# Differential heads in a fixed order, with spread transposes and ScalarE's sums of squares, and x added to the projection's first half by transfers

## The chip, the cores and the metric

The kernel runs on one core of a Trainium2 chip. The metric is the time of one execution in device microseconds (us). The kernel before took 655.91 us, the median of three runs (654.86 to 656.41). A profile of one execution gives each engine's instructions. TensorE (PE) multiplies matrices and transposes; VectorE (DVE), ScalarE (ACT) and GpSimd (POOL) work on tiles; SyncE's queue (SP) starts transfers. Matmuls write PSUM, which is used here as eight banks of 128 x 512 floats.

## The reference

One residual block on x, 512 tokens of 1024 features, all in float32:

```python
h = rms_norm(x, attn_norm_g)
z = h @ w_in                       # latent q, kv, rope key | differential q, k, v
y_mla  = mla_group(...)            # 8 heads of 64
y_diff = diff_group(...)           # 4 heads of 128
x = x + concat([y_mla, y_diff]) @ w_out
x = x + conv_ffn(rms_norm(x, ffn_norm_g), ...)
x = x + sigmoid(rms_norm(x, ple_norm_g) @ w_ple_gate) * (p @ w_ple_proj)
```

A differential head has two maps of logits, m = 0 and 1, each from 64 features. Both get the same bias by distance and a mask by chunks of 64 tokens. The head's output is `(softmax(l0) - lam * softmax(l1)) @ v`, and each token's 128 outputs are then divided by their root mean square and scaled by a gain.

## The kernel before, in words

**Products in three parts.** TensorE multiplies in a reduced float32 (`F32R`). Each operand is split in a high half (a cast on ScalarE, `split` L183, L186; weights L148) and a low half (what the cast lost, on VectorE, L184, L187, L149). `mm3` (L152) adds three products: high by high, high by low, low by high. A weight comes through `load_w` (L143): a transfer of 512 KB into one of three `raw` tiles, a cast, a subtraction. There are five pairs of `hi` and `lo` tiles.

**Stages.** The projections of x come first, then the eight latent heads, then the four differential heads with most of the output projection, the rest of that projection, the feed-forward part and the gate. The change lies in the differential stage, from about 152 to 240 us of the span.

**The differential stage.** The loop at L767 goes over 16 places: head h of 4, query block t of 4. A place (h,t) has t + 1 key blocks, since later ones are masked. TensorE's order is the program's order:

- logits of the place two ahead, both maps (`diff_logits`, L662), each map in its own bank of tag `lg` (three banks);
- at t = 0, the transposes of the next head's keys (`diff_T(h + 1, 1)`, L654), and after the products of this place those of its queries (`diff_T(h + 1, 0)`);
- one or two filler units (`pump`, by the table `FILL_DIFF`);
- transposes of this place's probabilities (`probs_T`, L533) into a bank of tag `tp` (two banks, which all transposes of the stage share), copied to `pt` by ScalarE;
- products with the values of the place before (`diff_pv`, L685), into one bank `ob` for each head;
- at t = 2, the transposes of the head before's outputs, with their split (`y_split`, L613).

`diff_logits` also issues what follows from the logits. For each map VectorE adds the bias and takes the negated maximum (L675), and ScalarE the exponential with its sum (L676). VectorE then puts both maps together (reciprocal L680, factor L681, combination L682). The `pm` tiles that hold the maps are four.

At a head's end `diff_pv` squares its 512 columns on ScalarE (L696), copies them to `yd` (L697), sums the squares by token on VectorE (L699), takes a power on GpSimd (L704) and scales `yd` on VectorE (L706).

**The filler.** `wo_units` (L638) is the output projection as a generator. Its first half takes y blocks 0 to 3 (the latent heads): for eight blocks b of 128 output features, two units of two y blocks each; the finished block is added to x by VectorE (`add_x`, L631), which frees one of two `acc` banks. The second half takes y blocks 4 to 7: for b = 0 to 3 one unit with blocks 4 and 5 is in the filler. The rest comes after the loop in two rounds (L802 to L899). The first round takes blocks 4 to 6, beginning with block 6 for b = 0. The second adds block 7, which is the last head's. The tiles of x are loaded by SyncE's queue in the last latent head (`load_x`, L712).

**Order on the other engines.** PE is under `manual_schedule`: it runs in program order. For VectorE, ScalarE and GpSimd this holds only inside marked regions, and from L736 to L847 there is none: a planner orders their instructions by its own estimate of when each is ready. There a later weight's cast can run ahead of an earlier copy, and does. `issue_after` puts single instructions behind others by hand.

Of the kernel before, what the change touches and what calls it, by code (L numbers as in the profile page):

```python
# [62 lines left out]
FILL_DIFF = ((2, 1, 1, 1), (1, 1, 2, 1), (1, 2, 2, 1), (1, 1, 2, 2))  # L63
# [31 lines left out]
def hybrid_block(ctx: ExitStack, tc: tile.TileContext, a: dict, out: bass.AP):  # L95
# [537 lines left out]
    wo2 = {}  # L633

    def wo_w(kq, dq):
        return load_w(a["w_out"][kq, dq], 1024, f"o{kq}{dq}")

    def wo_units(kq, dqs, nk):  # L638

        for dq in dqs:  # L640
            w = wo_w(kq, dq)
            if kq:
                wo2[dq] = w
            for b in (2 * dq, 2 * dq + 1):
                ps = bank("acc", f"o{kq}{b}")
                for k in range(0, nk, 2):
                    mm3(ps, wo_blocks(4 * kq + k, 4 * kq + k + 2, b, w), k == 0, k == nk - 2)
                    if k == nk - 2:
                        add_x(b, ps)
                    yield  # L650
# [3 lines left out]
    def diff_T(h, c):  # L654
        ps = bank("tp" if h else "acc", f"d{c}T{h}")
        for t in range(NT):
            TE.transpose(ps[:, tsl[t]], zd[c][t][:, h * P:(h + 1) * P], ident)
        h_, l_ = st[4 * (h % 2) + 2 * c], st[4 * (h % 2) + 2 * c + 1]
        split(h_, l_, ps, dcol if c == 0 else None)
        df["qk", h, c] = (h_, l_)  # L660

    def diff_logits(h, t):  # L662
# [3 lines left out]
        s0 = df["s0", h][:, t:t + 1]  # L666
        (qh_, ql_), (kh_, kl_) = df["qk", h, 0], df["qk", h, 1]
        pms, s1 = [], sm.tile([P, 1], F32, tag="s1", bufs=4, name="s1")
        for m in range(2):
# [3 lines left out]
            pm = pm_tile("pmd")  # L673
            nm = sm.tile([P, 1], F32, tag="nm", bufs=4, name="nmd")
            V.tensor_tensor_reduce(out=pm[:, :n], in0=ps[:, :n], in1=strips[0][:, h, T - n:], scale=1.0, scalar=3e38, op0=ALU.add, op1=ALU.min, accum_out=nm)  # L675
            S.activation(pm[:, :n], pm[:, :n], AF.Exp, bias=nm, scale=-1.0, accum_out=s0 if m == 0 else s1)  # L676
            pms.append(pm)

        cf = sm.tile([P, 1], F32, tag="cf", bufs=4, name="cf")
        V.reciprocal(cf, s1)  # L680
        V.scalar_tensor_tensor(cf, cf, nlam, s0, op0=ALU.mult, op1=ALU.mult)  # L681
        V.scalar_tensor_tensor(pms[0][:, :n], pms[1][:, :n], cf, pms[0][:, :n], op0=ALU.mult, op1=ALU.add)  # L682
        df["pm", h, t] = pms[0]

    def diff_pv(h, t):  # L685
        if t == 0:
            df["po"] = bank("ob", f"do{h}")
        po, pt = df["po"], df.pop(("pt", h, t))
        for j in range(t + 1):
            TE.matmul(po[:, tsl[t]], pt[:, tsl[j]], zd[2][j][:, h * P:(h + 1) * P], start=j == 0, stop=j == t)  # L690
        if t < NT - 1:
            return
        s0 = df["s0", h]
        yn = tt(f"yd{h}")
        sq = sq_tile("sqo")[:, :T]
        S.activation(sq, po, AF.Square)  # L696
        df["copy"] = S.copy(yn, po)  # L697
# [7 lines left out]
        yv = yn.rearrange("p (t d) -> p t d", d=P)  # L705
        df["scale"] = V.tensor_tensor(yv, yv, ro.unsqueeze(2).broadcast_to([P, NT, P]), op=ALU.mult)  # L706
        df["y", h] = yn
# [4 lines left out]
    def load_x():  # L712
# [3 lines left out]

    last_mla = [
        lambda: diff_T(0, 0),
        lambda: diff_T(0, 1),
# [42 lines left out]
    diff_logits(0, 0)  # L762
    mla_pv(*slots[-1])
    diff_logits(0, 1)
    pump()
    y_split(3, ymn[3], None, "tp")
    for i, (h, t) in enumerate(dslots):  # L767
        if i + 2 < len(dslots):
            diff_logits(*dslots[i + 2])
        if h + 1 < DH and t == 0:  # L770
            diff_T(h + 1, 1)
# [4 lines left out]
        if h + 1 < DH and t == 0:  # L776
            diff_T(h + 1, 0)
        if h and t == 2:
            y_split(4 + h - 1, df["y", h - 1], ocol, "tp")
# [10 lines left out]
    for dq in (2, 3):  # L790
        wo2[dq] = wo_w(1, dq)

    pk = kvp.tile([P, 4, 1024], F32R, tag="kv", name="pk")
    for i, (src, name) in enumerate(((a["pT"], "pT"), (a["w_pp"][0], "pp0"))):
        raw = load_raw(src, 1024, name)
        S.copy(pk[:, 2 * i], raw)
        with tc.issue_after(df["scale"].ins):
            V.tensor_tensor(pk[:, 2 * i + 1], raw, _f32(pk[:, 2 * i]), op=ALU.subtract)
# [3 lines left out]
    for b in order[:6]:  # L802
        n = len(early)
        if n == 5:
            y_split(7, df["y", 3], ocol, "tp")
# [27 lines left out]
    def behind_head(src, tag, name, bufs=1):  # L833

        h_, l_ = (ffn.tile([P, 1024], F32R, tag=tag + j, bufs=bufs, name=f"{tag}{j}{name}") for j in "hl")
        with tc.issue_after(df["copy"].ins):
            df["hi"] = S.copy(h_, src)
        with tc.issue_after(df["scale"].ins):
            df["lo"] = V.tensor_tensor(l_, src, _f32(h_), op=ALU.subtract)
        return h_, l_  # L840

    gu = lambda f, c0, c1: a["w_gu"][f][:, 512 * c0:512 * c1]
    rpp = raw_w(a["w_pp"][1], "rS", "pp1", bufs=3)
    W = {0: {0: behind_head(raw_w(gu(0, 0, 2), "rA", 0, bufs=2), "wA", 0, bufs=2)}}
    wpp.append(behind_head(rpp, "wT", "pp1"))

# [593 lines left out]
```

## Time and profile before

| what | us |
|---|---|
| median of three runs | 655.91 |
| the profiled execution | 655.36 |
| its span, from the first to the last instruction | 653.5 |
| TensorE busy in the span | 642.6 |
| VectorE busy | 475.3 |
| ScalarE busy | 362.4 |
| GpSimd busy | 57.0 |

The profiled execution's time is its span and 1.86 us around it. A row of a view in order of time has the start, the duration, the engine, the line, the operation, what it writes and reads, the shapes and a count. Brackets hold the idle time of that engine ahead of it and what ended it. A row of groups ends in the busy time and the mean duration of one in ns. A row of waits has the waiting engine and line, whom it waited for, and the sum, the count and the longest. A row of a stretch has its ends, its length, then the busy time and count of PE, of its weight loads (PEld), of VectorE, ScalarE and GpSimd, then the granted TensorE clock as a share of full speed, the share of transfers and GB/s. A matmul is pipelined, so its recorded duration reaches beyond the start of the next; what one costs is the distance between starts.

### The profile page before, as it was taken

What the parts mean: (1) busy time and instruction counts of PE and PEld (TensorE: products, weight loads), DVE (VectorE), ACT (ScalarE), POOL (GpSimd) and SP (SyncE); (2) the same over time, 40 slices, a digit from 0 to 9 for tenths busy, and PEclk for the clock granted to TensorE, in tenths of its full rate; (3) what the DMA queues carried; (4) which work ended last, traced back from release to release, by engine and by line L of the source; (5) the groups of instructions that cost most, each with busy time, mean ns of one, the idle gap of its engine ahead of it and who ended that gap; (6) DMA issues with size and microseconds to landing.
All of it is one profiled execution on the core that took longest, in us unless ns stands there. A gap on an engine that the chain in (4) does not pass through costs nothing.

```text
span 653.5 us, 10266 instructions
## 1 busy us (share of the span) xinstructions
PE 642.6 (98%) x3932; PEld 569.8 (87%) x3932; DVE 475.3 (73%) x860; ACT 362.4 (55%) x631; POOL 57.0 (9%) x93
## 2 busy tenths in 40 slices
PE   9999999999998999999999999999999999999997
PEld 9988888888777787889999999999999999988886
DVE  6789587666877677888886767677767676759444
ACT  7787666457665445656554645554454545637211
POOL 1520040000000121000100000000001000000000
PEclk9999999999998999999999999999999999999999
DMA  8241224143110157536675646564646464542121
GB/s 308 89 162 46 84 82 161 66 135 123 33 34 2 64 178 241 150 93 172 173 207 136 182 114 178 119 190 128 179 112 178 114 177 113 178 129 62 35 80 49
DMA packets 29912, 82.63 MB, mean 126 GB/s; under 512 B 3100, under 2 KB 4124, under 8 KB 29736
## 3 DMA queue, kind: packets, MB, share of 16 engines
q1 hardware_dynamic: 23816, 69.17, 31.8%
q0 software_dynamic: 5616, 12.33, 10.8%
q8 instruction: 31, 0.51, 0.3%
q10 hardware_dynamic: 432, 0.49, 0.2%
q14 instruction: 17, 0.14, 0.1%
HBM read 77.77 MB, written 5.52 MB: 127 GB/s over the span
## 4 chain that ended last, share of the span: by engine, by line
PE 87%; DVE 6%; ACT 4%; DMA 1%; issue 1%; POOL 0%; ACTq 0%; POOLq 0%
PE dn L157 6%; PE dn L156 6%; PE dn L155 6%; PE gx L157 4%; PE gx L155 4%; PE gx L156 4%; PE g L155 4%; PE g L156 4%; PE g L157 4%; PE zd L155 3%; PE zd L157 3%; PE zd L156 3%; PE pg L155 2%; PE pg L157 2%; PE pg L156 2%; PE u L155 2%
## 5 line engine op out<-in xcount | busy, mean ns | idle before, releaser
L827 DVE TENSOR_TENSOR wSl<-rS,wSh 128x1024 fp32r<-128x1024 f32 x21 | 25.7, 1224 | 44.3 <-ACT wSh L823 44.2
L157 PE MATMUL dn<-ah,lo_dn 128*128 128x512 f32 x144 | 56.4, 392 | 0.0
L156 PE MATMUL dn<-al,hi_dn 128*128 128x512 f32 x144 | 56.3, 391 | 0.0
L155 PE MATMUL dn<-ah,hi_dn 128*128 128x512 f32 x144 | 56.0, 389 | 0.0
L944 POOL DMA_DIRECT2D rS<-in_w_gu x19 | 22.7, 1194 | 251.0 <-DVE cv L1111 138.9
L823 ACT CAST wSh<-rS 128x1024 fp32r<-128x1024 f32 x21 | 22.1, 1051 | 35.6 <-PE gy L156 35.3
L155 PE MATMUL zd<-hi_d,xh 128*128 128x512 f32 x96 | 39.3, 410 | 0.0
L156 PE MATMUL zd<-lo_d,xh 128*128 128x512 f32 x96 | 37.6, 391 | 0.0
L631 DVE TENSOR_TENSOR x<-x,dn 128x512 f32<-128x512 f32 x44 | 29.9, 679 | 6.3 <-PE dn L157 6.1
L827 DVE TENSOR_TENSOR wTl<-rA,wTh 128x1024 fp32r<-128x1024 f32 x19 | 23.3, 1225 | 14.0 <-ACT wTh L823 13.4
L573 ACT ACTIVATE pm<-ml,nm,rq 128x128 f32<-128x128 f32 (+3 forms) x32 | 19.7, 617 | 22.6 <-DVE nm L571 22.6
L157 PEld LDWEIGHTS dn<-ah,lo_dn 128*128 128x128 f32 x144 | 27.0, 188 | 5.7
L156 PEld LDWEIGHTS dn<-al,hi_dn 128*128 128x128 f32 x144 | 27.0, 188 | 5.3
L155 PEld LDWEIGHTS dn<-ah,hi_dn 128*128 128x128 f32 x144 | 27.1, 188 | 5.2
L155 PE MATMUL o<-yh,hi_o 128*128 128x512 f32 x64 | 27.7, 432 | 1.0 <-DVE x L631 1.0
L676 ACT ACTIVATE pmd<-pmd,nmd 128x128 f32<-128x128 f32 (+3 forms) x32 | 17.9, 559 | 17.7 <-DVE nmd L675 17.7
L823 ACT CAST wAh<-rA 128x1024 fp32r<-128x1024 f32 x21 | 22.0, 1050 | 9.7 <-DMA rA<-in_w_gu 9.4
L1114 ACT ACTIVATE cv<-cv 128x512 f32<-128x512 f32 x22 | 13.9, 631 | 23.9 <-DVE cv L1111 23.8
L570 DVE TENSOR_REDUCE nm<-ml 128x1 f32<-128x128 f32 (+3 forms) x32 | 15.6, 487 | 15.1 <-PE ml L157 15.1
L155 PE MATMUL g<-b2h,wAh 128*128 128x256 f32 (+1 forms) x88 | 26.4, 300 | 0.2 <-ACT g L1067 0.2
L156 PE MATMUL g<-b2l,wAh 128*128 128x256 f32 (+1 forms) x88 | 26.2, 297 | 0.0
L157 PE MATMUL g<-b2h,wAl 128*128 128x256 f32 (+1 forms) x88 | 26.2, 297 | 0.0
(467 smaller groups left out, 2226.8 us busy)
## 6 DMA issues: line engine op xcount, KB each, us to landing
rA<-in_w_gu SPq DMA_DIRECT2D x22, 512.0 KB, 3.8
rS<-in_w_gu SPq DMA_DIRECT2D x22, 512.0 KB, 3.6
rS<-in_w_gu POOLq DMA_DIRECT2D x19, 512.0 KB, 6.0
raw_dn<-in_w_down SPq DMA_DIRECT2D x18, 512.0 KB, 5.9
raw_d<-in_w_d SPq DMA_DIRECT2D x12, 512.0 KB, 3.7
r<-in_w_gu SPq DMA_DIRECT2D x19, 256.0 KB, 6.1
raw_o<-in_w_out SPq DMA_DIRECT2D x8, 512.0 KB, 3.7
rS_pg<-in_w_pg SPq DMA_DIRECT2D x6, 512.0 KB, 4.0
```

The costliest lines, as they stand in the source:

```text
L155: TE.matmul(ps, xh, wh, start=first and i == 0, stop=False, skip_group_check=again)
L156: TE.matmul(ps, xh, wl, start=False, stop=False, skip_group_check=again)
L157: TE.matmul(ps, xl, wh, start=False, stop=last and i == n - 1, skip_group_check=again)
L570: V.reduce_max(nm, ps[:, :n], axis=AX.X, negate=True)
L573: S.activation(pm[:, :n], ps[:, :n], AF.Exp, bias=nm, scale=r, accum_out=mla["ssum", h // 2][:, t, h % 2:h % 2 + 1])
L631: V.tensor_tensor(xb(b), xb(b), ps, op=ALU.add)
L676: S.activation(pm[:, :n], pm[:, :n], AF.Exp, bias=nm, scale=-1.0, accum_out=s0 if m == 0 else s1)
L823: S.copy(h_, src)
L827: V.tensor_tensor(l_, src, _f32(h_), op=ALU.subtract)
L944: nc.gpsimd.dma_start(sums[f].rearrange("p (i c) -> p i c", i=2), a["w_gu"][f][:, :2048].rearrange("p (i c) -> p i c", i=2)[:, :, :512], a ...
L1114: S.activation(cv, cv, AF.Silu)
```

## The change: what it does

1. The planner has no part in the differential stage any more. A region with `manual_schedule` for VectorE, ScalarE and GpSimd begins behind the last latent head and goes on to where the next one began (L847); the `issue_after` edges there go.
2. `diff_logits` becomes `diff_mm`, `diff_max`, `diff_exp` and `diff_sum`, which the loop places by hand. In a place the order is: logits, maximum and exponential of map 0 of the place two ahead, the combination of the place one ahead, maximum of map 1, the high half of what was transposed at the end of the place before (`pend`), exponential of map 1, the low half.
3. Transposes are spread: queries of head h + 1 at the end of (h,0), keys of head h + 2 at the end of (h,2) (head 1's ahead of the loop), the outputs of head h - 1 at the end of (h,3). Their splits come in the place behind.
4. ScalarE sums the squares with `accum_out`, 128 columns in each place. The reduction on VectorE goes. The scaling of `yd` goes to GpSimd for heads 0 to 2, in place (h + 1,1).
5. In the first half of the projection ScalarE copies each block over the tile of x. When a tile's two blocks are in, a transfer from GpSimd's queue adds x from memory (`accum_op=ALU.add`). `load_x` stays as it is.
6. Casts and low halves of w_out stand at fixed places (`WO_HI`, `WO_LO`); only the first weight's are in the last latent head. `FILL_DIFF` has 19 units in place of 22, at most one for each place of the last head. The splits of `pT` and `w_pp` come behind the loop, and the low half of the feed-forward's first weight behind the first addition of the last round.

```diff
-FILL_DIFF = ((2, 1, 1, 1), (1, 1, 2, 1), (1, 2, 2, 1), (1, 1, 2, 2))
+FILL_DIFF = ((1, 2, 1, 1), (1, 2, 1, 1), (1, 2, 1, 1), (1, 1, 1, 1))
...
+    def wo_hi(kq, dq):
+        raw = load_raw(a["w_out"][kq, dq], 1024, f"o{kq}{dq}")
+        w = [wts.tile([P, 1024], F32R, tag=i, bufs=NW, name=f"{i}_o{kq}{dq}") for i in ("hi", "lo")]
...
+        df["wo", kq, dq] = (*hi(raw, w[0]), w[1])
...
-                        add_x(b, ps)
+                        if kq:
+                            add_x(b, ps)
+                        else:
+                            S.copy(xb(b), ps)
+                            if b % 2:
+                                i = b // 2
+                                nc.gpsimd.dma_start(x_sb[i].rearrange("p (k t) -> p k t", t=T), a["xT"][2 * i * P:(2 * i + 2) * P, :].rearrange("(k p) t -> p k t", p=P), accum_op=ALU.add)
...
+    def diff_exp(h, t, m):
+        n = (t + 1) * P
+        pm, nm = df["pm", h, t, m]
...
+        S.activation(pm[:, :n], pm[:, :n], AF.Exp, bias=nm, scale=-1.0, accum_out=df["s1", h, t] if m else df["s0", h][:, t:t + 1])
...
-        S.activation(sq, po, AF.Square)
-        df["copy"] = S.copy(yn, po)
-        sso = sm.tile([P, NT], F32, tag="sso", name="sso")
-        V.reduce_sum(sso, sq.rearrange("p (t d) -> p t d", d=P), axis=AX.X)
+        S.activation(sq_tile("sqo")[:, :P], po[:, tsl[t]], AF.Square, accum_out=df["sso", h][:, t:t + 1])
+        if t == NT - 1:
+            df["y", h] = tt(f"yd{h}")
+            S.copy(df["y", h], po)
...
+    def diff_norm(h, eng):
...
+        return lambda: eng.tensor_tensor(yv, yv, ro.unsqueeze(2).broadcast_to([P, NT, P]), op=ALU.mult)
...
+    region = tc.manual_schedule(engines={mybir.EngineType.DVE, mybir.EngineType.Activation, mybir.EngineType.Pool})
+    region.__enter__()
...
-    y_split(3, ymn[3], None, "tp")
+    pend = [y_T(3, ymn[3], None)]
+    for x in pend:
+        split(*x)
+    pend = [diff_T(1, 1)]
+    WO_HI = {0: (0, 1), 3: (0, 2), 6: (0, 3), 9: (1, 0), 11: (1, 1), 13: (1, 2), 15: (1, 3)}
+    WO_LO = {1: (0, 1), 4: (0, 2), 8: (0, 3), 10: (1, 0), 12: (1, 1), 14: (1, 2)}
     for i, (h, t) in enumerate(dslots):
...
+        new = dslots[i + 2] if i + 2 < len(dslots) else None
+        if new:
+            diff_mm(*new)
+            diff_max(*new, 0)
+            diff_exp(*new, 0)
+        if i + 1 < len(dslots):
+            diff_sum(*dslots[i + 1])
+        if new:
+            diff_max(*new, 1)
+        for x in pend:
+            split_hi(*x)
+        if new:
+            diff_exp(*new, 1)
+        for x in pend:
+            split_lo(*x)
+        if h and t == 1:
+            scale = diff_norm(h - 1, G)
+        if i in WO_LO:
+            wo_lo(*WO_LO[i])
         pump(FILL_DIFF[h][t])
         df["pt", h, t] = probs_T(df.pop(("pm", h, t)), t, f"d{h}{t}", True)
         if i:
             diff_pv(*dslots[i - 1])
...
+        if i in WO_HI:
+            wo_hi(*WO_HI[i])
+        if h and t == 1:
+            scale()
+        pend = []
+        if t == 0 and h + 1 < DH:
+            pend.append(diff_T(h + 1, 0))
+        if t == 2 and h + 2 < DH:
+            pend.append(diff_T(h + 2, 1))
         if h and t == 3:
+            pend.append(y_T(4 + h - 1, df["y", h - 1], ocol))
             if h == 2:
                 fill.append(wo_units(1, range(2), 2))
-    pump()
+    for x in pend:
+        split(*x)
     diff_pv(*dslots[-1])
+    scale = diff_norm(DH - 1, V)
+    wo_lo(1, 3)
     pump(100)
```

`split_hi` and `split_lo` are the two lines of `split`, apart; `y_T` and the new `diff_T` issue the transposes alone and hand back what a split needs; `wo_lo` is the low half of a weight.

More of the change, by code (lines that the diff above doesn't have):

```diff
@@ L658, in diff_T, with split_hi, split_lo, y_T @@
         h_, l_ = st[4 * (h % 2) + 2 * c], st[4 * (h % 2) + 2 * c + 1]
-        split(h_, l_, ps, dcol if c == 0 else None)
         df["qk", h, c] = (h_, l_)
-    def diff_logits(h, t):
+        return h_, l_, ps, dcol if c == 0 else None
+    def split_hi(h_, l_, src, col):
+        if col is None:
+            S.copy(h_, src)
+        else:
+            S.activation(h_, src, AF.Identity, scale=col)
+    def split_lo(h_, l_, src, col):
+        if col is None:
+            V.tensor_tensor(l_, src, _f32(h_), op=ALU.subtract)
+        else:
+            V.scalar_tensor_tensor(l_, src, col, _f32(h_), op0=ALU.mult, op1=ALU.subtract)
+    def y_T(i, src, col, tag="tp"):
+        ps = bank(tag, f"yT{i}")
+        for t in range(NT):
+            TE.transpose(ps[:, tsl[t]], src[:, tsl[t]], ident)
+        yh[i], yl[i] = th_tile(f"yh{i}")
+        return yh[i], yl[i], ps, col
+    def diff_mm(h, t):
         n = (t + 1) * P
@@ L715, in load_x @@
             nc.sync.dma_start(x_sb[i].rearrange("p (k t) -> p k t", t=T), a["xT"][2 * i * P:(2 * i + 2) * P, :].rearrange("(k p) t -> p k t", p=P))
+    wo_first = []
     last_mla = [
-        lambda: diff_T(0, 0),
-        lambda: diff_T(0, 1),
+        lambda: (split(*diff_T(0, 0, "acc")), wo_first.append(load_w(a["w_out"][0, 0], 1024, "o00"))),
+        lambda: split(*diff_T(0, 1, "acc")),
         lambda: (y_split(0, ymn[0], None, "acc"), y_split(1, ymn[1], None, "acc"), load_x()),
@@ L804, in hybrid_block @@
         if n == 5:
-            y_split(7, df["y", 3], ocol, "tp")
+            split(*y_T(7, df["y", 3], ocol))
         early[b] = bank("acc" if n < 2 else "lg" if n < 5 else "tp", f"o3{b}")
@@ L831, in hl @@
         return lo_(*hi_(*x, **k))
[L833 to L840, printed above, removed]
     gu = lambda f, c0, c1: a["w_gu"][f][:, 512 * c0:512 * c1]
     rpp = raw_w(a["w_pp"][1], "rS", "pp1", bufs=3)
-    W = {0: {0: behind_head(raw_w(gu(0, 0, 2), "rA", 0, bufs=2), "wA", 0, bufs=2)}}
-    wpp.append(behind_head(rpp, "wT", "pp1"))
-    region = tc.manual_schedule(engines={mybir.EngineType.DVE, mybir.EngineType.Activation, mybir.EngineType.Pool})
-    region.__enter__()
+    wpp.append(hl(rpp, "wT", "pp1"))
+    wA0 = hi_(raw_w(gu(0, 0, 2), "rA", 0, bufs=2), "wA", 0, bufs=2)
+    W = {0: {0: wA0[:2]}}
     nr_ = [ffn.tile([P, 1024], F32, tag="raw", bufs=2, name=f"nr{i}") for i in range(2)]
@@ L898, in hybrid_block @@
         sums_of(b)
-        held.close()
+        if b == 0:
+            lo_(*wA0)
     wts.release()
```

93 lines of the change are left out of this document (45 added, 48 removed).

## The prediction, made before the changed kernel was run

> **What bounds the kernel now.** I read the page's first part, then TensorE's waits from 150 to 260 us, where the changed code runs, and then the order of time around each of them.
>
> ```profile
> span 653.5 us, 10266 instructions
> PE 642.6 (98%) x3932; PEld 569.8 (87%) x3932; DVE 475.3 (73%) x860; ACT 362.4 (55%) x631; POOL 57.0 (9%) x93
> ```
>
> TensorE (PE) is busy for 642.6 of 653.5 us. The change takes no matmul away and adds none: transposes, logits, products with the values and projection blocks keep number and shape. So the other engines' saved work counts only where TensorE waits for it, and the prize is bounded by those waits:
>
> ```profile
> PE d0T L657 <- ACT pt L541: 1.7, 1, 1.7
> PE o L155 <- DVE x L631: 1.0, 1, 1.0
> PE yT L617 <- DVE st L184: 0.4, 1, 0.4
> PE nr L913 <- DVE nr L885: 0.4, 1, 0.4
> PE pTm L538 <- ACT pm L573: 0.2, 1, 0.2
> ```
>
> The largest, in order of time, with what the clock did behind it (the column before the last two is the granted clock):
>
> ```profile
> 196.32 1.06 PE L690 MATMUL do<-zd,pt 128*128 128x128 f32 x8
> 198.76 0.26 ACT L541 COPY pt<-pTd 128x128 f32<-128x128 f32 x1
> 199.07 0.66 PE L657 MATMUL d0T<-ident,zd 128*128 128x128 f32 x4 [1.69 <-ACT pt L541]
> ...
> 200.00:202.00 2.00, 2.00 (x9) 1.35 (x6) 2.00 (x4) 0.58 (x1) 0.38 (x1) 0.61 0.00 0
> 202.00:204.00 2.00, 2.00 (x6) 1.56 (x5) 1.54 (x5) 0.00 (x1) 0.63 (x1) 0.54 0.00 0
> ```
>
> TensorE stands 1.69 us before head 3's query transposes, until ScalarE has copied the small pt and so freed a bank. Then its clock is at 0.61 and 0.54 for two stretches of 2 us: 2 x 0.39 + 2 x 0.46 = 1.70 us lost again. The wait of 1.0 us did not do that; it is a wait for an addition of x:
>
> ```profile
> 219.91 0.68 DVE L631 TENSOR_TENSOR x<-x,o 128x512 f32<-128x512 f32 x1
> ...
> 220.64 0.50 PE L155 MATMUL o<-yh,hi_o 128*128 128x512 f32 x1 [0.96 <-DVE x L631]
> ```
>
> **What goes.** The change puts head h+1's two transposes into different places and gives each place a filler. The late copy at 198.76 stood behind a cast of a projection weight; in the new order the cast stands behind the copy. So 1.69 + 1.70 go there. At 220.64 a place took two blocks whose additions VectorE had not reached; the last head now has one unit a place, and its additions come a place ahead: 0.96 goes. The two small waits (0.4 and 0.2) lie in the last latent head. There VectorE did this:
>
> ```profile
> 155.33 1.22 DVE L149 TENSOR_TENSOR lo_o<-raw_o,hi_o 128x1024 fp32r<-128x1024 f32 x1
> 156.46 0.15 DVE L571 TENSOR_TENSOR nm<-nm,rq 128x1 f32<-128x1 f32 x1
> 156.53 0.69 DVE L184 TENSOR_TENSOR st<-d1T,st 128x512 fp32r<-128x512 f32 x1
> ```
>
> A weight's low half of 1.22 us stands ahead of both things waited for, the negated maximum and the low half of head 0's keys. Only the first weight is left there; the others move behind it. I credit both waits, 0.45 + 0.24 = 0.69 (bounds 0 and 0.69). Together 1.69 + 1.70 + 0.96 + 0.69 = 5.04 us. The wait of nr at 245.9 follows the last addition and stays.
>
> **What comes: three waits out of the fixed order.** ScalarE and VectorE now take in each place (h,t): maximum, exponential, combination, maximum, and only then the high and low half of what was transposed at the end of the place before. How long such a split takes from the start of the logits I read off rows of three query blocks:
>
> ```profile
> 211.98 0.45 PE L155 MATMUL dl<-st 64*128 64x384 f32 x2
> 212.71 0.50 PE L155 MATMUL o<-yh,hi_o 128*128 128x512 f32 x1
> 213.51 0.39 PE L155 MATMUL o<-yh,hi_o 128*128 128x512 f32 x1
> 213.74 0.40 PE L156 MATMUL o<-yh5l,hi_o 128*128 128x512 f32 x1
> 214.21 0.27 PE L538 MATMUL pTd<-ident,pmd 128*128 128x128 f32 x1
> ...
> 212.80 0.56 DVE L675 CUSTOM_DVE_ANT_0 pmd<-dl,strip 128x384 f32<-128x384 f32 x1 [0.55 <-PE dl L157]
> 213.40 0.62 ACT L676 ACTIVATE pmd<-pmd,nmd 128x384 f32<-128x384 f32 x1 [0.48 <-DVE nmd L675]
> ...
> 196.13 0.62 ACT L676 ACTIVATE pmd<-pmd,nmd 128x384 f32<-128x384 f32 x1 [1.01 <-DVE nmd L675]
> 196.75 0.60 ACT L676 ACTIVATE pmd<-pmd,nmd 128x384 f32<-128x384 f32 x1
> ...
> L186 ACT ACTIVATE yh<-yT,ocol 128x512 fp32r<-128x512 f32 x3 | 2.1, 688 | 0.8 <-PE yT L617 0.8
> L187 DVE SCALAR_TENSOR_TENSOR yh5l<-yT,ocol,yh 128x512 fp32r<-128x512 f32 x1 | 0.7, 747 | 0.0
> L183 ACT CAST st<-d1T 128x512 fp32r<-128x512 f32 x3 | 1.7, 565 | 0.0
> ```
>
> From the start of the logits the maximum comes after 0.82 (211.98 to 212.80), the exponential after 1.42 (213.40), the next ScalarE instruction 0.62 later, at 2.04. A scaled high half ends at 2.73, its low half at 3.48. TensorE itself is through the logits after 0.73 and through one filler unit after 2.23 (212.71 to 214.21 is 1.50).
>
> Place (3,0). Its unit is the first of the second half of the projection, on y blocks 4 and 5, and block 5 was transposed at the end of place (2,3). Its high half is wanted at 0.73 + 0.80 = 1.53 (212.71 to 213.51), its low half at 1.76 (213.74), and that comes at 3.48: a wait of 1.7 us, in two pieces of 1.2 and 0.5 with one matmul between. It is a need for data, so I take the whole; if ScalarE is late from the cast ahead, it is 0.3 more, and if VectorE's maximum begins at the first half of the logits, 0.4 less.
>
> Place (0,0). Head 1's key transposes go ahead of the logits now, and its query transposes want a bank of two at 2.23 + 0.11 = 2.34. One bank comes free with the low half of the keys. VectorE, still at y block 3, begins 0.13 late: exponential at 1.55, high half 2.17 to 2.74, low half (0.69, the st row above) to 3.43. The wait is 1.1. Below, none, if the bank comes otherwise; above 1.9, if it is the one that the copy of pt frees, behind a second exponential and a copy of x. In place (2,0) the values' products of 1.06 (the row at 196.32) stand ahead as well, and 3.40 against 3.48 leaves 0.1.
>
> Behind the last place. Y block 6 is transposed there, two places later than before, and the next block of the projection begins with it.
>
> ```profile
> 223.34 0.60 PE L538 MATMUL pTd<-ident,pmd 128*128 128x128 f32 x4
> 223.78 2.14 PE L690 MATMUL do<-zd,pt 128*128 128x128 f32 x14
> 225.67 0.48 PE L155 MATMUL o<-yh,hi_o 128*128 128x512 f32 x1
> 225.99 0.39 PE L156 MATMUL o<-yh6l,hi_o 128*128 128x512 f32 x1
> 225.95 0.60 ACT L696 ACTIVATE sqo<-do 128x512 f32<-128x512 f32 x1 [1.25 <-PE do L690]
> L148 ACT CAST hi_o<-raw_o 128x1024 fp32r<-128x1024 f32 x3 | 3.1, 1042 | 0.0
> L676 ACT ACTIVATE pmd<-pmd,nmd 128x128 f32<-128x128 f32 x8 | 3.2, 400 | 5.5 <-DVE nmd L675 5.5
> ```
>
> Counted from the last probabilities' transposes (223.34): four transposes 0.44, six value matmuls at 1.89/14 = 0.135 to 1.25, four transposes to 1.69, eight value matmuls to 2.77; the low half of block 6 is wanted at 2.77 + 0.32 = 3.09. ScalarE squares the 128 columns from 1.25 + 0.28 = 1.53 (225.67 to 225.95; 0.40 as an exponential of that width, with its sum), casts the last weight (1.04) to 2.97, takes the high half to 3.66, VectorE the low half to 4.41. The wait is 1.3. If the cast finds room before the square it is 0.3; I take the order as written.
>
> New waits: 1.7 + 1.1 + 0.1 + 1.3 = 4.2 us, between 1.7 (1.3, none, 0.1, 0.3) and 5.3 (2.0, 1.9, 0.1, 1.3) by these bounds.
>
> **What costs nothing, and its cover.** The first row below has the stage in one piece; its busy times are those of PE, PEld, DVE, ACT and POOL. Sixteen squares of 0.40 in place of four of 0.60, eight copies of a block (0.58 by the row of yd) and two casts more (1.04; seven of w_out where three of it and two of pk stood) put 4.0 + 4.6 + 2.1 = 10.7 us on ScalarE, which is idle for 66 - 39.6 = 26 us of it; the copies of pt behind them are wanted a place later, some 4 us. VectorE loses eight additions, three scalings and four reductions, and gets four of the weights' low halves (1.22 each) in. Its fullest place is (3,0): the low half of block 5 to 3.48, a weight's to 4.7, an addition to 5.4; the bank that this frees is used next in place (3,2), some 8 us after the start. GpSimd's scaling of y is bounded by its own additions; the transfer that adds x by one of the same kind:
>
> ```profile
> 160.00:226.00 66.00, 63.20 (x393) 50.32 (x393) 51.32 (x152) 39.59 (x104) 3.05 (x3) 0.97 0.09 27
> ...
> L697 ACT COPY yd<-do 128x512 f32<-128x512 f32 x4 | 2.3, 581 | 0.0
> L880 POOL TENSOR_TENSOR nr<-nr,nsq 128x512 f32<-128x512 f32 x3 | 4.2, 1403 | 10.0 <-ACT nsq L878 9.9
> rS<-in_w_gu POOLq DMA_DIRECT2D x19, 512.0 KB, 6.0
> ```
>
> The scaling (1.4, behind a power and at most one transfer's issue) has two places, over 5 us, before the transposes that read it. A transfer lands in 6.0 us; the first reader of the tiles that come last is 20 us behind. If one were late, the addition holds a bank, and the price is its lateness; I see none. The plain loads of x stay, on a queue that stands idle then.
>
> **Sum.** 4.2 - 5.04 = -0.8 us. The profiled execution took 655.36 us (span 653.5), 0.55 under the median of the runs, 655.91. So 654.5 for its like, and 655.1 for the median. I take about 0.2%, 1.3 us, as what a measurement here can tell from no change: 655.1 is no change.
>
> The clock is the open term. A wait of 1.69 us was followed by half clock, one of 0.96 was not; the new waits of 1.1, 1.3 and 1.7 in two pieces lie between, so I add nothing, and hold 1.70 each for the range. The Trainium skill, page TensorE: Matmul & The Clock Gate, section What's actually happening, has the clock halve after at least one idle window of about 3.4 us; this trace differs, as 1.69 us were enough. By that rule the fall would not hang on these waits at all, and would not go with the old one: -0.8 + 1.70 = +0.9 us, again no change.
>
> **The rivals.** First, faster: the new waits are mostly covered. The bank in place (0,0) comes free early and the cast behind the last place finds room: -5.04 + 1.7 + 0.3 = -3.0, so 652.9; with no new wait at all 650.9. For it: the 26 us in which ScalarE idles, and that splits before the change were often taken without a wait. Against it: the wait in (3,0) hangs on data alone. Chance 0.39, as the bounds of the new waits reach down to 1.7.
>
> Second, slower: the clock falls behind the new waits as it did behind the old. The place is the matmuls behind (3,0) and behind (0,0) or the last place; the price 1.70 each; it decides between 0.96 and 1.69 us of idleness close together. One fall gives 656.8, still no change; two give 658.5. Chance of two, or of one with waits at their upper bounds: 0.20.
>
> Third, the change does not do what it says for TensorE: the old wait comes back in place (2,0) because the bank there is that of pt, copied behind two exponentials, a split and a copy of x. That adds 0.6 and no more, 655.7; it sits inside the forecast.
>
> **How the numbers follow.** No change, 654.6 to 657.2, has 0.41 and its likeliest value is 655.1. Faster by over 0.2% has 0.39, slower 0.20. The range leaves out the case without any new wait below and two full falls above: 652.2 to 658.0.
>
> **What would show it.** Right: TensorE's waits lose the d0T of 1.7 and the o behind x, and gain an o behind yh5l of about 1.7 at the start of the last head, a d0T in the first of about 1.1, an o behind yh6l of about 1.3 behind the last. The granted clock between 150 and 240 us shows whether one of them cost more. Wrong: these waits missing, or new ones on VectorE's additions, on a transfer into x, or on GpSimd's scaling.

## The result, and the profile after

The changed kernel takes 658.48 us (median of 7 runs, 657.25 to 659.26) against 655.76 us of the kernel before (7 runs, 654.63 to 657.53) on the same chip: 1.0046 times as long, 95% interval 1.003 to 1.0063. It is 2.7 us slower. The forecast was no change.

The profiled execution took 658.42 us. First its span and the first row of its page, then TensorE's waits from 150 to 260 us:

```profile
span 656.6 us, 10307 instructions
...
PE 644.1 (98%) x3932; PEld 570.3 (87%) x3932; DVE 468.8 (71%) x845; ACT 368.6 (56%) x667; POOL 67.8 (10%) x100
```

```profile
PE o L155 <- ACT yh L678: 1.5, 1, 1.5
PE d0T L669 <- DVE st L682: 1.4, 1, 1.4
PE d0T L669 <- DVE yh4l L684: 0.4, 1, 0.4
PE nr L985 <- DVE nr L959: 0.4, 1, 0.4
PE o L155 <- ACT yh L186: 0.4, 1, 0.4
PE yT L689 <- DVE st L682: 0.3, 1, 0.3
PE do L735 <- ACT sqo L736: 0.3, 1, 0.3
PE o L156 <- DVE yh5l L684: 0.3, 1, 0.3
PE o L156 <- DVE yh6l L187: 0.3, 1, 0.3
```

The two large waits of before (1.69 before head 3's query transposes, 0.96 behind an addition of x) are gone. In their place stand the waits that were forecast, and two that were not (`yT` 0.3, `do` 0.3). The wait of `nr` (0.4) stood there before too. The largest, in place (3,0), in order of time on three engines:

```profile
211.19 0.45 PE L155 MATMUL dl<-st 64*128 64x384 f32 x2
...
212.07 1.05 ACT L298 CAST hi_o<-raw_o 128x1024 fp32r<-128x1024 f32 x1
212.26 0.39 PE L156 MATMUL o<-yh4l,hi_o 128*128 128x512 f32 x1
212.49 0.39 PE L157 MATMUL o<-yh,lo_o 128*128 128x512 f32 x1
213.01 0.63 ACT L717 ACTIVATE pmd<-pmd,nmd 128x384 f32<-128x384 f32 x1
213.59 0.56 DVE L709 CUSTOM_DVE_ANT_0 pmd<-dl,strip 128x384 f32<-128x384 f32 x1
213.62 0.69 ACT L678 ACTIVATE yh<-yT,ocol 128x512 fp32r<-128x512 f32 x1
214.34 0.75 DVE L684 SCALAR_TENSOR_TENSOR yh5l<-yT,ocol,yh 128x512 fp32r<-128x512 f32 x1 [0.19 <-ACT yh L678]
214.36 0.49 PE L155 MATMUL o<-yh,hi_o 128*128 128x512 f32 x1 [1.49 <-ACT yh L678]
215.15 0.79 PE L156 MATMUL o<-yh5l,hi_o 128*128 128x512 f32 x1 [0.29 <-DVE yh5l L684]
```

Y block 5 was transposed a place earlier. On ScalarE its high half stands behind a weight's cast and an exponential, on VectorE its low half stands behind both maxima. TensorE needs both. The rows also show what such a wait costs. Neighbouring matmuls start 0.23 apart (212.26, 212.49). From 212.49 to 214.36 it is 1.87, so 1.64 are lost where 1.49 are recorded as idle; from 214.36 to 215.15 it is 0.79, so 0.56 where 0.29 are recorded. Behind this place the clock falls (0.72, 0.50 and 0.93 in the rows below):

```profile
214.00:216.00 2.00, 1.35 (x3) 0.91 (x4) 1.81 (x4) 0.96 (x3) 0.00 (x0) 0.72 1.08 138
216.00:218.00 2.00, 2.00 (x10) 1.82 (x8) 0.92 (x2) 0.27 (x1) 0.00 (x0) 0.50 0.97 170
218.00:220.00 2.00, 2.00 (x12) 1.25 (x11) 0.78 (x3) 0.89 (x4) 0.00 (x0) 0.93 0.52 203
```

2 x (0.28 + 0.50 + 0.07) = 1.7 us lost, as much as behind the old wait.

**Where the time came from.** From head 0's query transposes to the start of `nr` it was 93.18 us before (152.69 to 245.87) and is 96.08 now (153.18 to 249.26): 2.90 more. By distances between starts, as above, the waits of the changed part now cost 1.5 in place (0,0), 0.5 in (1,3), 0.55 in (2,0), 2.2 in (3,0), 0.45 in (3,2) and 1.1 behind the last place: 6.3. The old ones cost 1.85 and 1.15, and the last latent head now loses 0.65 less. 6.3 - 3.65 = 2.65, and one fall of the clock against one. That is the loss, within 0.25.

The executions without a profile agree. In all 20 profiles a mean clock of 0.998 or more goes with no fall, and one of 0.997 or less with one or two. Of the change's seven executions two have 0.999 (657.25 and 657.33 us) and five 0.996 to 0.997 (median 658.94). Of the kernel before, timed 117 times beside the experiments on several chips, 57 have 0.998 or more (median 654.43) and 47 have 0.996 to 0.997 (median 656.21). So at like clock the change is slower by 2.7 to 2.9 us: the loss is that of the waits. The fall in the kernel before does not come in every execution.

### The profile page after: what moved, and what is told of

Same layout as the page of the kernel before. It is cut to its first block, busy times and chain, and to the rows that moved or that the text cites. A ratio compares the mean times of both kernels' runs of the same rounds, so it can differ in the third digit from the quotient of the medians.

```text
span 656.6 us, 10307 instructions
## 1 busy us (share of the span) xinstructions
PE 644.1 (98%) x3932; PEld 570.3 (87%) x3932; DVE 468.8 (71%) x845; ACT 368.6 (56%) x667; POOL 67.8 (10%) x100
## 4 chain that ended last, share of the span: by engine, by line
PE 60%; DVE 2%; ACT 1%; issue 0%; ACTq 0%
PE dn L157 6%; PE dn L156 6%; PE dn L155 6%; PE gx L157 4%; PE gx L155 4%; PE gx L156 4%; PE g L155 4%; PE g L157 4%; PE g L156 4%; PE pg L155 2%; PE pg L157 2%; PE pg L156 2%; PE u L155 2%; PE u L157 2%; PE u L156 2%; PE gy L156 1%
## 5 line engine op out<-in xcount | busy, mean ns | idle before, releaser
L912 DVE TENSOR_TENSOR wAl<-rA,wAh 128x1024 fp32r<-128x1024 f32 x22 | 26.8, 1218 | 0.7 <-ACT wAh L908 0.7
L709 DVE CUSTOM_DVE_ANT_0 pmd<-dl,strip 128x128 f32<-128x128 f32 (+3 forms) x32 | 15.6, 490 | 15.6 <-PE dl L157 13.6
```

Source lines behind the costliest of these rows:

```text
L709: V.tensor_tensor_reduce(out=pm[:, :n], in0=df.pop(("ps", h, t, m))[:, :n], in1=strips[0][:, h, T - n:], scale=1.0, scalar=3e38, op0=ALU.a ...
```

## The experiments

Each kernel was timed beside the kernel before. The medians of before differ from one timing to another (654.9 to 655.8), so the ratio decides.

| kernel | us | ratio, 95% interval | TensorE's waits of 0.5 and more in the changed part |
|---|---|---|---|
| the change | 658.48 | 1.0046, 1.003 to 1.0063 | 1.5, 1.4 |
| 1 splits first | 661.67 | 1.0097, 1.0078 to 1.0116 | 1.5, 1.2, 1.0, 0.7 |
| 2 filler later | 657.79 | 1.0039, 1.0024 to 1.0053 | 2.0, 1.4 |
| 3 x by VectorE | 660.08 | 1.0062, 1.0042 to 1.0083 | 1.5, 1.4, 0.8 |
| 4 square over the head | 658.15 | 1.0029, 1.0011 to 1.0047 | 1.4, 1.3 |
| 5 planner orders | 657.75 | 1.0031, 1.0015 to 1.0047 | 1.7, 1.3, 0.7 |
| 6 before, transfers of x | 659.34 | 1.0053, 1.0036 to 1.0071 | 2.3, 2.2, 1.6, 1.0 |
| 7 before, TensorE's order | 653.35 | 0.9967, 0.9949 to 0.9986 | none |
| 8 outputs earlier | 657.81 | 1.0033, 1.0019 to 1.0047 | 1.6, 1.3, 0.6 |
| 9 fixed order alone | 661.30 | 1.0078, 1.0051 to 1.0104 | 2.0, 1.4, 1.4, 0.7 |
| 10 planner, no transfers | 658.09 | 1.0044, 1.0026 to 1.0061 | 1.6, 1.3, 0.7 |
| 11 TensorE's order, transfers | 660.12 | 1.0061, 1.0037 to 1.0085 | 3.7, 0.5 |
| 12 as 8, scaling on VectorE | 659.29 | 1.0057, 1.0038 to 1.0076 | 1.6, 1.0, 0.6, 0.6 |
| 13 split between maxima | 652.75 | 0.9964, 0.9951 to 0.9977 | 0.7 |
| 14 as 11, gate's cast held | 651.46 | 0.9943, 0.9922 to 0.9963 | none |
| 15 as 9, order of 13 | 654.99 | 1.0008, 0.9992 to 1.0024 | 0.7, 0.6, 0.6, 0.5 |
| 16 as 13, two fillers first | 652.64 | 0.996, 0.9944 to 0.9975 | 0.5 |
| 17 cast moved alone | 656.07 | 1.0016, 1.0002 to 1.003 | 1.4, 1.1 |
| 18 split moved alone | 654.10 | 0.9995, 0.9982 to 1.0007 | 0.6 |

### 1 to 4: the change with one thing altered

The first theory (A): the waits come because a split stands behind softmax steps. Against it: the units' places, the transfers, the squares.

1, both halves ahead of the maxima:

```diff
+        for x in pend:
+            split_hi(*x)
+            split_lo(*x)
         if new:
             diff_mm(*new)
             diff_max(*new, 0)
...
```

> The changed kernel with one thing moved: in each place both halves of what was transposed in the place before come ahead of the first maximum and the first exponential, not behind them. Theory A (the fixed order makes TensorE wait for splits that stand behind the softmax steps): the d0T waits of 1.4 and 0.4 us and the yT wait of 0.3 go, the o wait in the last head's first place shrinks from 1.5 + 0.3 to under 1.0 because only the cast of a weight is still ahead, and the clock no longer falls; 5 us less than the changed kernel's 658.4, so 652.5 to 655. Theory B (ScalarE's added squares and copies make everything late, whatever the order): the waits stay or move, under 1 us less.

2, the place with y block 5 gets no filler, and the next place two units:

```diff
-FILL_DIFF = ((1, 2, 1, 1), (1, 2, 1, 1), (1, 2, 1, 1), (1, 1, 1, 1))
+FILL_DIFF = ((1, 2, 1, 1), (1, 2, 1, 1), (1, 2, 1, 1), (0, 2, 1, 1))
```

> The changed kernel with the last head's filler table (0, 2, 1, 1) in place of (1, 1, 1, 1): the first unit of the projection's second half comes one place later, when y block 5 is long split. Theory A: the o waits of 1.5 and 0.3 go, worth 2.2 us from start to start, and with them the fall of the clock behind them, 1.7 us; 3.9 us less, about 654.5. If the fall does not hang on that wait: 2.2 less and a granted clock that still falls near 215 us. Theory B: the wait comes back elsewhere in the last head, under 1 us less.

3, `add_x` for both halves of the projection, no copy and no transfer:

```diff
-                        if kq:
-                            add_x(b, ps)
-                        else:
-                            S.copy(xb(b), ps)
...
+                        add_x(b, ps)
```

> The changed kernel with x added by VectorE as before; ScalarE's eight copies and the four adding transfers go. Theory A: these copies stand behind the splits and ahead only of copies wanted a place later, so less than 0.5 us either way, and the d0T wait of 1.4 and the o wait of 1.5 stay. Theory B (load of ScalarE): 4.6 us less on ScalarE gives 1.5 us or more back. Theory C (the transfers or GpSimd disturb the others): the same gain, with shorter instructions on VectorE.

4, one square of 512 columns at a head's end with VectorE's reduction, as before the change:

```diff
-        S.activation(sq_tile("sqo")[:, :P], po[:, tsl[t]], AF.Square, accum_out=df["sso", h][:, t:t + 1])
         if t == NT - 1:
+            df["sq", h] = sq_tile("sqo")[:, :T]
+            S.activation(df["sq", h], po, AF.Square)
...
+        V.reduce_sum(sso, df["sq", h].rearrange("p (t d) -> p t d", d=P), axis=AX.X)
```

> The changed kernel with one square of 512 columns at a head's end and the sum on VectorE, as before the change. Theory A: only the wait of a value product for the square of the place before (0.3, in the last head) goes, so 0 to 0.6 us less, and the three large waits stay. Theory B (load of ScalarE): 4 us less on ScalarE gives 1 us or more back.

None beats the kernel before. The first is slower still, against theory A as I had it. Its order of time in head 0:

```profile
170.32 1.05 ACT L298 CAST hi_o<-raw_o 128x1024 fp32r<-128x1024 f32 x1
171.26 0.70 ACT L678 ACTIVATE st<-d0T,dcol 128x512 fp32r<-128x512 f32 x1
172.00 0.75 DVE L684 SCALAR_TENSOR_TENSOR st<-d0T,dcol,st 128x512 fp32r<-128x512 f32 x1 [2.95 <-ACT st L678]
172.66 0.68 DVE L709 CUSTOM_DVE_ANT_0 pmd<-dl,strip 128x512 f32<-128x512 f32 x1
174.86 1.22 DVE L302 TENSOR_TENSOR lo_o<-raw_o,hi_o 128x1024 fp32r<-128x1024 f32 x1
176.14 0.50 PE L157 MATMUL o<-yh,lo_o 128*128 128x512 f32 x1 [1.52 <-DVE lo_o L302]
```

VectorE, in a fixed order, stands 2.95 us before a low half whose high half is behind a cast on ScalarE. Everything after it is late, and TensorE then waits for a weight. In the second, VectorE reaches an addition of x late (2.0 us at 222.06): the wait on y block 5 is gone, but the place with two units brings back a wait of the kind that the kernel before had at 220.64. In the third VectorE has the additions again; it is 1.6 us slower than the change by the medians, though the intervals of the ratios overlap, and nothing in it speaks for the transfers as the cause. The fourth gains little, again within overlapping intervals. So the waits travel along the line, and taking off one of these loads alone does not end them.

### 5 to 7, 9 to 11: the parts, with the planner and without

The letters get a new meaning here. A: the fixed order loses. B: TensorE's own new order loses. C: the copies and transfers of x, with ScalarE's added work, lose.

5 begins the fixed region where it began before the change; the rest of the change stays.

```diff
     wo[0, 0] = wo_first[0]
-    region = tc.manual_schedule(engines={mybir.EngineType.DVE, mybir.EngineType.Activation, mybir.EngineType.Pool})
-    region.__enter__()
     diff_mm(0, 0)
...
```

> The changed kernel, but from the first differential logits to the start of the feed-forward part the planner again orders VectorE, ScalarE and GpSimd (the region with the fixed order begins where it began before). TensorE's new order, the squares by place, the transfers of x and the scaling on GpSimd stay. Theory A (the loss is made by the fixed order: a split, a cast or a square stands in line ahead of what TensorE waits for): TensorE's waits of 1.4 to 1.5 us go, 654 to 656 against 658.5 for the change. Theory B (the loss is made by TensorE's own new order, which asks for a split too soon): the waits before d0T and o stay about where they are, 658 to 659.5. Theory C (the loss is ScalarE's added work and the transfers): also 658 or more, with other waits on ScalarE.

6 is the kernel before with the copies and transfers of x in `wo_units`:

```diff
-                        add_x(b, ps)
+                        if kq:
+                            add_x(b, ps)
+                        else:
+                            S.copy(xb(b), ps)
...
```

> The kernel before with one part of the change: in the projection's first half ScalarE copies the block and a transfer from GpSimd's queue adds x; the planner and TensorE's order stay. Theory A: the wait of 0.96 us on an addition of x may go or stay, as it lies in the second half's units too: 654.5 to 656, no difference that can be told. Theory C: slower by over 1.3 us, 657 or more.

7 is the kernel before with TensorE's new order and the new `FILL_DIFF`:

```diff
+    diff_T(1, 1)
     for i, (h, t) in enumerate(dslots):
...
-        if h + 1 < DH and t == 0:
-            diff_T(h + 1, 1)
...
+        if t == 2 and h + 2 < DH:
+            diff_T(h + 2, 1)
         if h and t == 3:
+            y_split(4 + h - 1, df["y", h - 1], ocol, "tp")
...
```

> The kernel before with TensorE's new order alone: the transposes at the ends of other places and the new table of filler units; the planner orders the other engines. Theory A (the fixed order alone is at fault): the d0T wait of 1.69 us with its 1.70 us of half clock goes and little comes, 652.5 to 655. Theory B (TensorE's order is at fault): 657 to 659, with the wait on y block 5 at the start of the last head.

9 is the change with the edits of 3 and 4 and the scaling on VectorE, 10 is 5 with the edit of 3, 11 is 7 with the edit of 6. The line new in 9:

```diff
-            scale = diff_norm(h - 1, G)
+            scale = diff_norm(h - 1, V)
```

> The changed kernel with VectorE's additions of x, one square over a whole head with VectorE's reduction, and the scaling on VectorE, as before the change: so TensorE's new order and the fixed order of the other engines (with the weights' casts and low halves at their places) are what is left of the change. TensorE's new order alone took 653.35. Theory A (the fixed order holds splits behind other work): 657 to 660, with the waits on y block 5 and before head 1's queries. Theory C (the transfers, the squares and GpSimd's scaling make the loss): 652.5 to 655.

> The changed kernel with the planner in place of the fixed order (657.75), and now also x added by VectorE and not by transfers; squares by place, scaling on GpSimd and the weights' places stay. Theory C (with the planner it is the copies and transfers of x that lose): 652.5 to 655, the waits o behind x and nr (1.7 and 1.3) gone. Theory D (squares by place and GpSimd's scaling lose): 657 to 658.5.

> The kernel before with TensorE's new order (653.35) and the copies and transfers of x, planner kept. If the copies and transfers cost by themselves what they cost in the old order (3.7 us): 656.5 to 658. If they cost only where transposes for two heads follow each other, as in the old order: 652.5 to 654.5.

TensorE's order alone makes the kernel faster by 0.33%: theory B is out. The fixed order on top of it (9) takes 661.3 against 653.35, even more than theory A had. TensorE's waits in 9:

```profile
PE o L155 <- ACT yh L672: 2.0, 1, 2.0
PE yT L683 <- DVE st L676: 1.4, 1, 1.4
PE d0T L663 <- DVE st L676: 1.4, 1, 1.4
```

5 and 10 did not free the change of its loss, against theory A's numbers: the old waits for splits are nearly gone, but there are others behind the loop, in 5 with a fall of the clock of twice the usual length (246 to 254 us):

```profile
PE nr L985 <- DVE nr L959: 1.7, 1, 1.7
PE o L155 <- DVE x L631: 1.3, 1, 1.3
```

These two kernels lack the `issue_after` edges too, which in the kernel before hold later weights' casts back; so they do not undo the fixed order cleanly, and I take nothing from their times, though 10 lies in the range of theory D.

6 and 11 surprised me: in the planner's order the copies and transfers cost 3.7 and 6.8 us (6.2 by the ratios of 11 and 7). The order of time of 11, then the same cast in 7:

```profile
196.75 1.04 ACT L801 CAST pk<-raw_pp 128x1024 fp32r<-128x1024 f32 x1 [2.95 <-DMA raw_pp<-in_w_pp]
197.70 0.58 ACT L183 CAST st<-d1T 128x512 fp32r<-128x512 f32 x1
...
199.15 1.09 PE L617 MATMUL yT<-ident,yd 128*128 128x128 f32 x4 [3.74 <-DVE st L184]
```

```profile
193.50 1.05 ACT L795 CAST pk<-raw_pp 128x1024 fp32r<-128x1024 f32 x1 [0.64 <-DMA raw_pp<-in_w_pp]
```

The planner had placed the cast of a weight of the gate's part (`w_pp`) ahead of a split. Its load, issued at 190.74 right behind a transfer of x at 189.55, landed after 6.0 us; in 7 it took 3.7. ScalarE stood 2.95 us and TensorE 3.74, and the clock was at half for some 7 us. In 6 ScalarE stands the same way before both casts, 2.21 us for `pT` and 2.78 for `w_pp`, and TensorE's waits of 2.2 and 2.3 follow these two.

### 8 and 12: transposing the outputs a place earlier

In 8 the outputs are transposed at the end of a head's third place and the keys at the end of its fourth; the first place has two units, the square is that of 4. 12 is 8 with the scaling on VectorE, by the line shown for 9.

```diff
-FILL_DIFF = ((1, 2, 1, 1), (1, 2, 1, 1), (1, 2, 1, 1), (1, 1, 1, 1))
+FILL_DIFF = ((2, 1, 1, 1), (1, 2, 1, 1), (1, 2, 1, 1), (1, 1, 1, 1))
...
-        if t == 2 and h + 2 < DH:
+        if h and t == 2:
+            pend.append(y_T(4 + h - 1, df["y", h - 1], ocol))
+        if t == 3 and h + 2 < DH:
             pend.append(diff_T(h + 2, 1))
         if h and t == 3:
-            pend.append(y_T(4 + h - 1, df["y", h - 1], ocol))
```

> The changed kernel with three edits: outputs of the head before are transposed at the end of a head's third place and the keys of the head after next at the end of its fourth (the other way round in the change); head 0's first place takes two filler units and its second two (20 in all); one square over a whole head and VectorE's reduction, as before the change. In the fixed order the split of y blocks 4 to 6 then comes a place ahead of its use. If the waits are those that I take them for (a split wanted in the place in which it is made), the wait in the last head's first place (2.2 us start to start), that behind the last place (1.1), that before head 1's queries (1.5) and the half clock of 1.7 go: 658.5 less 6.5, 652 to 654. If they travel to another place, as with the splits put first: 656 to 660.

> The kernel with outputs transposed earlier (657.81; its largest waits, 1.6 and 1.3 us, were for GpSimd's scaling of y) with the scaling on VectorE. If those waits are all that is left of the loss: 657.8 less 2.9 and 0.2 for each start, 654 to 655. If VectorE's line is then too long and holds the next split, 657 or more.

The waits for splits go, and others come. In 8 GpSimd's line has a power and a transfer's issue ahead of the scaling:

```profile
192.45 1.21 POOL L660 DMA_DIRECT2D x<-in_xT  x1
193.25 1.48 POOL L751 TENSOR_TENSOR yd<-yd,ro 128x512 f32<-128x512 f32 x1
194.79 0.66 PE L689 MATMUL yT<-ident,yd 128*128 128x128 f32 x4 [1.28 <-POOL yd L751]
```

In 12 that wait is gone, a split is late by 1.6 and a factor by 1.0. Both misses: moving a step without looking at the line that it joins.

### 13 to 18: the order within a place

The theory then (A1): not that the order is fixed, but how it is within a place. 13 takes the order that the planner had chosen in 7. There, behind the transposes of y block 4 at 193.94, the high half comes at 195.91, the first maximum at 196.43, the low half at 196.91, the second maximum at 197.57, a weight's cast at 197.64 and the second exponential at 198.57:

```diff
         if new:
             diff_mm(*new)
-            diff_max(*new, 0)
-            diff_exp(*new, 0)
+        for x in pend:
+            split_hi(*x)
         if i + 1 < len(dslots):
             diff_sum(*dslots[i + 1])
         if new:
-            diff_max(*new, 1)
+            diff_max(*new, 0)
+            diff_exp(*new, 0)
         for x in pend:
-            split_hi(*x)
+            split_lo(*x)
         if new:
+            diff_max(*new, 1)
+        if i - 1 in WO_HI:
+            wo_cast(*WO_HI[i - 1])
+        if new:
             diff_exp(*new, 1)
-        for x in pend:
-            split_lo(*x)
```

`wo_cast` is the cast out of `wo_hi`, which keeps the load. 15 is 9 with this order; 16 is 13 with the table of 8 and the square of 4; 17 has the cast's move alone, 18 the split's. 14 is 11 with one edit, which holds two casts (`pT` and `w_pp`) behind the last head's copy:

```diff
-        S.copy(pk[:, 2 * i], raw)
+        with tc.issue_after(df["copy"].ins):
+            S.copy(pk[:, 2 * i], raw)
```

> The changed kernel, still in a fixed order, but with the order in a place that the planner chose in the faster kernel: high half first, combination of the next place, maximum and exponential of map 0, low half, maximum of map 1, the weight's cast (from the end of the place before to here), exponential of map 1. Theory A1 (the order within a place makes the loss): the waits on y block 5 (1.5) and before d0T (1.4) shrink under 0.5 each, with them the fall of the clock: 658.5 less 2.6, 0.4 and up to 1.7, 653.5 to 655.5. Theory A2 (any fixed order is too stiff, waits travel as with the splits put first): 657 or more.

> The kernel of TensorE's new order with the copies and transfers of x (660.12), with one edge more: the two casts of pT and the gate's weight are held behind the last head's copy. If the transfers cost because ScalarE stands for those weights: 653 to 655, the wait of 3.7 us and the half clock of some 7 us behind it gone. If the copies on ScalarE cost by themselves: 657 or more.

> The fixed order alone (661.3: additions of x, reduction and scaling on VectorE) with the order within a place as in the run of the split between maxima. A1: 653 to 656, since VectorE's load is that of the faster kernel. A2, or VectorE's load: 657 or more.

> The split between the maxima, with two filler units in the first place (as before the change) and one square over a whole head: the wait before head 1's queries gets 1.5 us more cover, and no product with the values waits for a square. A1: 0.5 to 1.5 us under the run without these two edits. A2: the same or more.

> The changed kernel with the weight's cast moved from the end of a place to between the exponentials of the next, the split left behind the maxima. If the cast makes the waits (it stood ahead of map 0's exponential at y block 5's wait): 653 to 655. If the split's place behind both maxima makes them: 656.5 to 658.5, the wait on y block 5 shorter by at most the part of 1.04 us that is not covered.

> The changed kernel with the split's high half first and its low half between the maxima, the cast left at the end of a place. If the split's place makes the waits: 653 to 655. If the cast makes them (it stands right ahead of the high half then): 656.5 or more, with waits of about 1 us where a cast and a split meet, as with both halves put first.

13 takes 652.75 us, ratio 0.9964: with all of the change's loads and transfers it is 0.8% faster than the change (1.0046) and faster than the kernel before. Place (3,0) in it, and its two waits for splits:

```profile
210.95 0.45 PE L155 MATMUL dl<-st 64*128 64x384 f32 x2
211.46 0.69 ACT L682 ACTIVATE yh<-yT,ocol 128x512 fp32r<-128x512 f32 x1
211.78 0.56 DVE L713 CUSTOM_DVE_ANT_0 pmd<-dl,strip 128x384 f32<-128x384 f32 x1 [0.46 <-PE dl L157]
212.26 0.75 DVE L688 SCALAR_TENSOR_TENSOR yh5l<-yT,ocol,yh 128x512 fp32r<-128x512 f32 x1
212.38 0.61 ACT L721 ACTIVATE pmd<-pmd,nmd 128x384 f32<-128x384 f32 x1 [0.24 <-DVE nmd L713]
212.93 0.55 DVE L713 CUSTOM_DVE_ANT_0 pmd<-dl,strip 128x384 f32<-128x384 f32 x1
213.00 1.03 ACT L298 CAST hi_o<-raw_o 128x1024 fp32r<-128x1024 f32 x1
213.06 0.50 PE L156 MATMUL o<-yh5l,hi_o 128*128 128x512 f32 x1 [0.19 <-DVE yh5l L688]
```

```profile
PE d0T L673 <- DVE st L686: 0.7, 1, 0.7
...
PE o L156 <- DVE yh5l L688: 0.2, 1, 0.2
```

The high half begins 0.51 after the logits (2.43 in the change, 213.62 against 211.19); it uses the time in which ScalarE would wait for the first maximum anyway. The low half stands between the maxima, when its high half is there; nothing idles for it as in 1. The cast goes where no one waits for it.

17 and 18 share this out: the cast's move alone takes the ratio from 1.0046 to 1.0016, the split's to 0.9995, together 0.9964. -0.0030 and -0.0051 add up to nearly the -0.0082 of both. The split's part is clear of noise, and so is the cast's on top of it (13 against 18); the cast's alone is not quite, as the interval of 17 just touches that of the change. 17's time lies between its two forecasts, just below the one by which the split's place makes the waits. In 17 the wait in (3,0) is still there, shorter:

```profile
212.94 0.50 PE L155 MATMUL o<-yh,hi_o 128*128 128x512 f32 x1 [1.07 <-ACT yh L682]
```

15 and 13 were timed together: 654.99 and 652.75, intervals of the ratios apart. So under a good order the transfers, squares by place and GpSimd's scaling together are worth 2.2 us. VectorE is busy for 54.47 us from 160 to 226 in 15 and for 48.80 in 13, which fits; no run separates the three. 15 also sets a limit to the theory: with the additions of x, the reduction and the scaling on VectorE as in 7 it is still 0.4% behind 7, the intervals apart. The order within a place gives back most of what 9 lost, not all; what the rest is stays open. 16 adds nothing that can be told.

14 takes 651.46, the best here, though its interval overlaps those of 7, 13 and 16. The wait of 3.7 is gone; what is left from 150 to 260 us begins with

```profile
PE yT L617 <- DVE st L184: 0.4, 1, 0.4
PE nr L919 <- DVE nr L891: 0.4, 1, 0.4
```

so the loss of 11 came from the two casts' place in the planner's order, and by the row of 3.74 mostly from that of `w_pp`.

## Why the prediction was wrong, point by point

**The bound: right.** TensorE is busy for 98%, and only its waits counted. ScalarE's busy time from 160 to 226 us rose from 39.59 to 45.16 (to 49.17 in 13, which is faster):

```profile
160.00:226.00 66.00, 61.84 (x376) 48.38 (x376) 46.48 (x139) 45.16 (x135) 12.08 (x10) 0.97 0.35 73
```

```profile
160.00:226.00 66.00, 64.63 (x405) 50.94 (x405) 48.80 (x146) 49.17 (x146) 12.94 (x11) 1.00 0.38 86
```

The first row is the change, the second is 13, which gets through more of its work in the same stretch. In 13 the added load costs nothing that can be told. In the change it was not quite free: a square costs 0.45 in (3,2), as said below, and in (3,0) a copy of x and a square run ahead of the late cast. But taking off the one (3) or the other (4) leaves the wait there at 1.5 and 1.3.

**What goes: right but for the clock.** Both waits went, and the last latent head lost 0.65 of the 0.69 credited. The 1.70 of half clock did not go: it stands behind (3,0) now. Nor was there such a fall to be taken from every execution: of 117 executions of the kernel before, timed beside the experiments, 57 had a mean clock of 0.998 or more.

**What comes: places right, sum too small.** By starts, as they were forecast: (3,0) 1.7 forecast and 2.2 real, since the cast ahead of the exponential did delay it, by 0.4 (exponential 1.82 after the logits, 1.42 forecast; the bound had 0.3 for that); (0,0) 1.1 and 1.5, within its bounds; (2,0) 0.1 and 0.55; behind the last place 1.3 and 1.1. Not priced at all: 0.5 for a bank in (1,3), and 0.45 in (3,2), where a square on a head's shared bank holds the next product with the values. Together 4.2 and 6.3, which is above the upper bound of 5.3 too. The recorded idle time of these waits is only 4.8 (1.49 + 1.36 + 0.4 + 0.37 and four of 0.3): each costs 0.15 to 0.3 more than it shows, and there are eight pieces in place of two large ones. No wait in the change is for a transfer or for the scaling, as forecast.

**The failed step: "so I add nothing" for the clock, and the sizes of the new waits.** The sum was -0.8. The fall that was credited away came back (+1.7). The waits cost 6.3 where 4.2 were forecast, and those that went 3.65 where 3.34 were credited: +1.8. That makes +2.7, the measured difference. The rival that came nearest is the slower one. Its number for two falls, 658.5, fits by luck: there was one fall, and the rest came from waits above their upper bound.

**What I did not see at all** is that the order within a place was the choice that decided. I took the waits as the price of the spread transposes. They were that of one order: by 13 most of them need not come, and by 7 TensorE's new order is itself a gain of 0.33%. The rows of before had shown the better order already, in splits that were taken without a wait; the prediction names them only as evidence for its faster rival.

**The clock rule.** The prediction set beside the sum a rule by which the fall would not hang on these waits. The Trainium skill, page TensorE: Matmul & The Clock Gate, section What's actually happening, asks for an idle window of about 3.4 us for the lower clock. The trace does not agree: nothing here idled as long as 3.4 us but 11, and 1.07 in 17 was followed by a fall. The same section says that full clock comes back after a busy window of about 3.4 us; with that the trace agrees, as every fall but two costs 1.7 us, which at half clock (0.50 from 216 to 218 us in the change) is 3.4 us; those of 5 and 11 cost twice that.

## What to carry to other kernels

When the planner is taken away and the order is written by hand, ask of each instruction what stands right ahead of it on its engine, and who waits behind; copy the planner's order of a good run as a start. Put a step where its engine would wait anyway (a high half while the maximum is being taken), and work that no one waits for behind what someone does. A part that loses alone may only have joined a badly ordered line: here the same transfers cost 6.8 us with two casts ahead of urgent steps, and nothing that can be told with these casts held back.

## What the runs showed of the hardware

- A wait's recorded length alone does not decide whether the clock falls. In 20 profiles (before, the change, 18 experiments) TensorE waited 1.0 us or more 29 times behind the start-up. Nine of these waits, of 1.07 to 3.74 us, had the half clock with or behind them; twenty, of 1.00 to 2.35, had not. Three of 6 were 2.22, 2.35 and 1.56, with full clock throughout. Why one falls and another does not stays open.
- Six of the 20 profiled executions have such a fall at 22 to 27 us, the other fourteen have none. It costs the same 1.7 us. Executions of one kernel differ by about as much with their mean clock: the nine of 13 with 0.998 or more have a median of 652.69, the three below 654.28. Where the falls of those without a profile lay is not recorded.
- A load of 512 KB (`w_pp`) that took 3.6 us from issue to landing in the kernel before and 3.7 in 7 took 6.0 in 11, 5.9 in 6 and 5.7 in 14, each time about 1.2 us behind a transfer that adds into x. That the adding makes the difference is not shown: in the kernel before a load of `w_out` behind four plain loads of x took 5.9.
